# Later, source-ordered splits of two summed operands of the output projection, and one small step of the tail moved

## The chip, the core and the metric

The kernel runs on one core of a Trainium2 chip. The metric is the device time of one launch in microseconds; of several runs the median is given. TensorE is called PE, VectorE DVE, ScalarE ACT, GpSimd POOL and SyncE SP, as in the profile.

## The reference

A trunk of two layers over 1024 tokens of width 1024. The first is a gMLP layer with chunks of 128 tokens; the second is attention in a sliding window of 128 tokens, with 16 query heads of size 64 on 4 shared key/value heads, sinks and ALiBi. The change touches only the second layer's end. Cut to that:

```python
q, z = jnp.split(h @ w_in, 2, axis=-1)
# per block of 128 tokens: logits = q k^T + alibi, masked to the window
p = jnp.exp(logits - m[..., None])
denom = jnp.sum(p, axis=-1) + jnp.exp(sink - m)
o = einsum(p, v) / denom
y = (o * jax.nn.silu(z)) @ w_out
h = h + rms_norm(y, b_post_g)
```

Everything is float32.

## The kernel before, in words

*Products.* A float32 operand is split into a high part (an ACT copy to fp32r, L105) and a low part (a DVE subtraction, L106). `mm3` (L215 to L218) then makes three fp32r matmuls: high by high, high by low, low by high. The large products use Strassen's scheme with seven block products instead of eight, so sums and differences of operand blocks have to be formed and split too.

*Stages.* First the gMLP layer (v, then u and z, then its output projection), then q, the first half of z, the keys and values. After that, `attn` runs 16 units of attention (8 blocks of tokens in two groups p of heads) and weaves into them, in small steps, a list of other PE work called `fill`: the rest of z and q, and at the end `Out.early`, the first five block products of the output projection. `Out.late`, the last two block products and the finals, runs after the units.

*A unit.* `scores` makes the logits of 8 heads in four PSUM banks with the tag "s" (matmuls L1155), then on DVE masks each bank (L1162, COPY_PREDICATED) and takes bias and row maximum twice per bank (L1169, tile mx). `exps` runs on ACT (L1175), `normalise` on DVE in two halves (L1181, L1182, tile pr), `transposes` on PE (L1189, tile pt), with ACT copies (L1191) and POOL selections (L1194, L1195). `values` multiplies by v (L1218, tile o, again two "s" banks, so it needs banks that the masks and maxima have set free), and `gate` multiplies by z on DVE (L1230, L1231). There are four "s" banks in all.

*The output projection.* In `early` the products go in the order oc (twice), od, oe with the summed operand o1, oe with o7. Each product has 8 steps (two weight blocks u, four token blocks t), so there are 40 steps, numbered from 0: od is steps 16 to 23, the o1 product 24 to 31, the o7 product 32 to 39. Each step is six matmuls.

*The two summed operands.* o1 and o7 each hold four token blocks. For each block, the plan SUMS names (m, t, step of the load, step of the sum, step of the split): the gated output of a unit of the first four blocks is loaded again from memory (`y_again`, a raw tile), POOL adds that of a unit of the last four blocks (L253), and the sum is split into o1 or o7. Source order of the steps is the order of this table, but the scheduler may move instructions on an engine; `held` ties the instructions of the units on DVE and ACT to their source order, and leaves those of `fill` free. o1 and o7 lie in the space of q's first half (tags P0a and P0b), which the oc products read.

*Raw buffers.* The raw tiles (tag "raw") have three buffers. They are shared by the loads for o1 and o7, by the two weight blocks of product 3 that are split on the chip (w46 and w47, from wo_b; the other output weights were split earlier and kept in memory), and by three of the residual loads for the finals. The sums for o1 go to another tile, so their raw tile is free after the sum; those for o7 stay in the raw tile until the split.

*The tail.* `late` makes product of (L216 to L218, tile of) in two parts, and for each token block adds, scales by the gain on DVE or POOL, and finishes with the residual (L1309). ef holds the mean squares: four columns are prepared at once (L1447, 128x4), then one per token block (L1461).

Of the kernel before, what the change touches and what calls it, by code (L numbers as in the profile page):

```python
# [7 lines left out]
F32 = mybir.dt.float32  # L8
# [3 lines left out]
AF = mybir.ActivationFunctionType  # L12
ALU = mybir.AluOpType

P = 128
D = 1024
# [8 lines left out]
EPS = 1e-6  # L25
# [25 lines left out]
def tile_yoco(  # L51
# [19 lines left out]
    nc = tc.nc  # L71
# [9 lines left out]
    def bank(tag, name):  # L81
        return psum.tile([P, 512], F32, tag=tag, name=name)
# [21 lines left out]
    def split(hi, lo, src):  # L104
        nc.scalar.activation(hi, src, AF.Copy)  # L105
        nc.vector.tensor_tensor(lo, src, hi.bitcast(F32), ALU.subtract)  # L106
# [19 lines left out]
    class Weights:  # L126
# [30 lines left out]
        def load(self, i):  # L157
            for n in range(min(len(self.raw), 20), min(i, 19) + 1):
                src, kind = self.order[n]
                if n < 20:  # L160
                    self.raw[n] = wload(src, f"w{n}")
# [48 lines left out]
    def wnext():  # L210
        w = weights.get()
        weights.ahead()
        return w
# [38 lines left out]
    def add(out, a, b, op, eng=None):  # L252
        (eng or nc.vector).tensor_tensor(out, a, b, op)  # L253
# [820 lines left out]
    def by_head(t):  # L1074

        return t.rearrange("p k t -> p (k t)").rearrange("p (m b g t) -> p m b g t", m=4, g=2, t=P)
# [204 lines left out]
    ORDER = "01FavFbgmtpFFn"  # L1281
    lags = {}
    BY = [6, 12, 19, 25, 32, 38, 45, 51, 57, 64, 71, 78, 85, 92, 99, 106, 112, 120]
    SUMS = [(1, 0, 0, 2, 17), (1, 1, 3, 5, 18), (1, 2, 6, 8, 19), (7, 0, 8, 11, 18), (1, 3, 10, 12, 20), (7, 1, 14, 16, 21), (7, 2, 19, 21, 24), (7, 3, 23, 25, 28)]
    behind = {}

    def held(what, *args):
# [31 lines left out]
    def y_again(p, t):  # L1319
        r = raw_tile(f"y{p}_{t}_{len(again)}")  # L1320
        again[len(again)] = r
        load(r[:, 0:512], yd[p][t])
        return r[:, 0:512]

    class Out:
# [26 lines left out]
        def sums(self, plan):  # L1352
            todo = {}
            for m, t, *at in plan:
                for what in range(3):
                    todo.setdefault(at[what], []).append((what, m, t))
            raw = {}
            for at in range(max(todo) + 1):
                for what, m, t in todo.get(at, ()):
                    if what == 0:  # L1360
                        raw[m, t] = y_again(m == 1, t)
                    elif what == 1:
                        d = self.s1[t] if m == 1 else raw[m, t]
                        mix = [a.rearrange("p (a t) -> p a t", t=P) for a in (d, raw[m, t])]
                        add(mix[0], mix[1], self.z[0][:, :, t * P:(t + 1) * P], ALU.add, nc.gpsimd)
                        raw[m, t] = d
                    else:
                        if m not in self.o:
                            self.o[m] = big.tile([P, 2, 4, 4, P], F32R, tag={1: "P0a", 7: "P0b"}[m], name=f"o{m}")
                        split(*(self.o[m][:, e, t].rearrange("p m t -> p (m t)") for e in range(2)), raw[m, t])  # L1370
                yield

        def early(self):
# [31 lines left out]
            def products():  # L1405
                ps = [bank("mm", f"oc{t}") for t in range(4)]
                yield from self.product(ps, self.of(self.q0, 0), True, True, lambda t, p: copy(m4[t], p))
                yield from self.product(ps, self.of(self.q0, 1), False, True, after2)
                ps = [bank("mm", f"od{t}") for t in range(4)]
                yield from self.product(ps, self.of(self.q1, 0), True, True, after5)  # L1410
                ps = [bank("mm", f"oe{t}") for t in range(4)]
                yield from self.product(ps, sum_operand(1), True, True,
                                        lambda t, p: add(n2[t], n2[t], p, ALU.add))
                yield from self.product(ps, sum_operand(7), False, True, after7)

            sums = self.sums(SUMS)
            for _ in products():
                step(sums)
                yield

        def late(self):
            gp, n2, m5, q1 = self.gp, self.n2, self.m5, self.q1
            ps = [bank("s", f"of{t}") for t in range(4)]

            def after3(t, p):
                c = m5[t]
                add(c, c, p, ALU.add)
                self.square(1, 0, t, c)
                add(c, c, gp[0], ALU.mult, nc.gpsimd)

            for k, _ in enumerate(self.product(ps, self.of(q1, 1), True, False, after3)):
                if k < 4:
                    d = self.z[1][:, :, k * P:(k + 1) * P]
                    hi, lo = (by_head(w)[:, 0:2, k] for w in q1)
                    split(hi, lo, d.rearrange("p (m g) t -> p m g t", m=2))
                elif k == 4:
                    w = [wnext() for _ in range(2)]
                    for dst, src in self.stores:
                        tc.keep_in_program_order(nc.sync.dma_start(out=dst, in_=src))
                elif k == 5:  # L1440
                    final(*self.rest.pop(0))
                elif k == 6:
                    hf = big.tile([P, 4, D], F32, tag="P0a", name="hf1")
                    xt = [load(hf[:, t], h1d[1][t]) for t in range(4)]
            final(*self.rest.pop(0))
            ef = const.tile([P, 8], F32, tag="rpa", name="ef1")
            nc.vector.tensor_scalar(ef[:, 0:4], self.ss[1][:, 0], 1.0 / D, EPS, ALU.mult, ALU.add)  # L1447
            y = self.of(q1, 0)
            for t in range(4):
                for m in range(4):  # L1450
                    hi, lo = w[m // 2]
                    cs = slice(m % 2 * 512, m % 2 * 512 + 512)
                    a = y(t, m)
                    mm3(ps[t], a[0], a[1], hi[:, cs], lo[:, cs], False, m == 3)
                c, o, r = n2[t], self.m4[t], ef[:, 4 + t:5 + t]
                add(c, c, ps[t], ALU.add)
                self.square(1, 1, t, c)
                add(o, c, gp[1], ALU.mult)
                if t:
                    final(*self.rest.pop(0))  # L1460
                nc.vector.tensor_scalar(r, self.ss[1][:, 1, t:t + 1], 1.0 / D, ef[:, t:t + 1], ALU.mult, ALU.add)  # L1461
                nc.gpsimd.tensor_tensor(r, r, nhalf[:, 0:1], ALU.pow)
                self.rest.append((1, t, [m5[t], o], r, xt[t]))
            final(*self.rest.pop(0))
# [85 lines left out]
```

## Time and profile before

| | |
|---|---|
| median of 3 runs | 1044.87 us (1043.71 to 1045.28) |
| the profiled execution | 1044.52 us |
| its span, first to last instruction | 1042.8 us |
| mean granted PE clock | 0.993 |
| PE busy | 1025.3 us (98%) |
| DVE busy | 792.4 us (76%) |
| ACT busy | 541.1 us (52%) |
| POOL busy | 276.2 us (26%) |

The span lies inside the execution's own time. A row of a timeline gives the start and the length in us, the engine, the line, the operation, the tiles written and read, and in brackets the idle time of the engine before it with what ended it. Where instructions follow each other without a wait, the next starts somewhat ahead of the end of the one before, since they overlap in the engine. A row with x2 merges two.

### The profile page before, as it was taken

The page shows a single profiled execution, that of the slowest core. Times are in us where ns is not written, and L with a number is a line of the kernel's source. Part 1 is how long each engine was busy: PE and PEld are TensorE (multiplying, and loading weights), DVE is VectorE, ACT ScalarE, POOL GpSimd, SP SyncE. Part 2 cuts the span into 40 slices and gives each one's busy share as a digit, 9 for nine tenths or more (in the row PEclk, how much of TensorE's full clock was granted, in tenths as well). Part 3 has the DMA queues.
Part 4 walks back from the last instruction along what each step waited for, and adds up shares of the span by engine and source line. Part 5 has one row for each costly group of instructions (what it writes and reads, how often), then busy time and mean ns, then how long its engine had stood idle before and what let it go on. Part 6 is the DMA issues. An engine that isn't in the chain of part 4 may idle for free.

```text
span 1042.8 us, 14527 instructions
## 1 busy us (share of the span) xinstructions
PE 1025.3 (98%) x5186; PEld 839.6 (81%) x5186; DVE 792.4 (76%) x1342; ACT 541.1 (52%) x1018; POOL 276.2 (26%) x257
## 2 busy tenths in 40 slices
PE   9999999999999999999999999999999999999896
PEld 7888788888888888888878888888987777777575
DVE  6987467899898998988697777655166658787778
ACT  6684444565665565755445465444145445556332
POOL 0000004384664755743200000000001113244244
PEclk9999999999999999999999999999999999999898
DMA  8877353445555455457998651996135544334465
GB/s 313 273 277 287 101 175 116 151 152 176 173 162 172 134 184 157 157 176 254 316 388 311 203 203 53 349 352 241 51 143 190 176 149 142 112 106 146 173 222 202
DMA packets 117672, 203.83 MB, mean 195 GB/s; under 512 B 7776, under 2 KB 59872, under 8 KB 117600
## 3 DMA queue, kind: packets, MB, share of 16 engines
q1 hardware_dynamic: 113088, 194.22, 54.4%
q10 hardware_dynamic: 4512, 8.68, 2.4%
q8 instruction: 41, 0.67, 0.3%
q14 instruction: 31, 0.25, 0.1%
HBM read 142.05 MB, written 60.82 MB: 195 GB/s over the span
## 4 chain that ended last, share of the span: by engine, by line
PE 74%; DVE 7%; DMA 7%; issue 5%; ACT 3%; POOL 2%; SPq 1%; POOLq 0%; DVEq 0%; ACTq 0%
PE qz L216 5%; PE ub L216 5%; PE ub L218 5%; PE ub L217 5%; PE qz L218 5%; PE qz L217 5%; PE sp L659 2%; PE uc L217 2%; PE uc L216 2%; PE uc L218 2%; PE o L1218 2%; PE s L1155 2%; PE ob L218 2%; PE ob L216 2%; PE ob L217 2%
## 5 line engine op out<-in xcount | busy, mean ns | idle before, releaser
L1175 ACT ACTIVATE pr<-pr,mx 128x129 f32<-128x129 f32 x128 | 50.2, 394 | 56.3 <-DVE mx L1169 56.2
L216 PE MATMUL qz<-n_hi,whi_w 128*128 128x512 f32 x192 | 77.3, 403 | 0.0
L218 PE MATMUL qz<-n_hi,wlo_w 128*128 128x512 f32 x192 | 75.1, 391 | 0.1
L217 PE MATMUL qz<-n_lo,whi_w 128*128 128x512 f32 x192 | 74.9, 390 | 0.0
L803 POOL TENSOR_TENSOR presum<-presum_raw 128x128 f32<-128x128 f32 x80 | 49.1, 645 | 91.9 <-DMA od<-presum 84.8
L110 DVE SCALAR_TENSOR_TENSOR wlo_w<-raw_w,gn,whi_w 128x512 fp32r<-128x512 f32 x40 | 28.7, 748 | 48.6 <-ACT whi_w L109 48.5
L109 ACT ACTIVATE whi_w<-raw_w,gn 128x512 fp32r<-128x512 f32 x40 | 27.1, 715 | 63.2 <-PE pv L218 30.4
L253 POOL TENSOR_TENSOR f<-raw_uz 128x512 f32<-128x512 f32 x15 | 20.3, 1356 | 124.4 <-DMA raw_uz<-in_wuz_in_dram 105.6
L1195 POOL TENSOR_SCALAR_AFFINE_SELECT pc<-pc 128x1024 f32<-128x1024 f32 x16 | 20.1, 1259 | 121.6 <-DVE wlo_w L110 108.8
L216 PE MATMUL ub<-T,uzhilo_g 128*128 128x512 f32 x128 | 50.7, 396 | 0.9 <-ACT uz_slots L256 0.9
L106 DVE TENSOR_TENSOR uzhilo_g<-f,uzhilo_g 128x1024 fp32r<-128x1024 f32 x31 | 47.3, 1526 | 5.4 <-ACT uzhilo_g L105 5.4
L216 PE MATMUL ub<-T,whi_g 128*128 128x512 f32 x128 | 50.8, 397 | 0.0
L812 DVE TENSOR_TENSOR presum<-presum 128x128 fp32r<-128x128 f32 x80 | 50.6, 681 | 0.1
L218 PE MATMUL ub<-T,wlo_g 128*128 128x512 f32 x128 | 50.0, 391 | 0.0
L218 PE MATMUL ub<-T,uzhilo_g 128*128 128x512 f32 x128 | 49.9, 390 | 0.0
L217 PE MATMUL ub<-T,uzhilo_g 128*128 128x512 f32 x128 | 49.9, 390 | 0.0
L217 PE MATMUL ub<-T,whi_g 128*128 128x512 f32 x128 | 49.9, 390 | 0.0
L105 ACT ACTIVATE uzhilo_g<-f 128x1024 fp32r<-128x1024 f32 x31 | 32.8, 1057 | 32.2 <-PE uc L218 25.9
L216 PE MATMUL uc<-T,uzhilo_g 128*128 128x512 f32 x124 | 49.0, 395 | 0.0
L256 ACT ACTIVATE uz_slots<-ub 128x512 f32<-128x512 f32 x48 | 28.2, 587 | 39.7 <-PE ub L218 37.4
L217 PE MATMUL uc<-T,uzhilo_g 128*128 128x512 f32 x124 | 48.3, 390 | 0.0
L218 PE MATMUL uc<-T,uzhilo_g 128*128 128x512 f32 x124 | 48.3, 390 | 0.0
(399 smaller groups left out, 3301.0 us busy)
## 6 DMA issues: line engine op xcount, KB each, us to landing
raw_uz<-in_wuz_in_dram SPq DMA_DIRECT2D x32, 512.0 KB, 3.7
td<-uz_slots SPq DMA_DIRECT2D x56, 256.0 KB, 2.2
orawP2a<-td SPq DMA_DIRECT2D x28, 512.0 KB, 4.3
od<-presum SPq DMA_DIRECT2D x16, 640.0 KB, 4.0
raw<-in_wv_in_dram SPq DMA_DIRECT2D x17, 512.0 KB, 5.5
vg<-vd SPq DMA_DIRECT2D x8, 1024.0 KB, 5.6
orawP2b<-in_wo_a_dram SPq DMA_DIRECT2D x16, 512.0 KB, 8.0
raw_w<-in_wqz_dram SPq DMA_DIRECT2D x16, 512.0 KB, 5.1
```

The source lines that it names most:

```text
L105: nc.scalar.activation(hi, src, AF.Copy)
L106: nc.vector.tensor_tensor(lo, src, hi.bitcast(F32), ALU.subtract)
L109: nc.scalar.activation(hi, src, AF.Copy, scale=g)
L110: nc.vector.scalar_tensor_tensor(lo, src, g, hi.bitcast(F32), ALU.mult, ALU.subtract)
L216: nc.tensor.matmul(out, lhsT=a_hi, rhs=b_hi, start=start, stop=False, skip_group_check=True)
L217: nc.tensor.matmul(out, lhsT=a_hi, rhs=b_lo, start=False, stop=False, skip_group_check=True)
L218: nc.tensor.matmul(out, lhsT=a_lo, rhs=b_hi, start=False, stop=stop, skip_group_check=True)
L256: nc.scalar.activation(out, a, AF.Copy)
L659: nc.tensor.matmul(psv[:, n], lhsT=d["vg"][:, 4 * j + n, i * P:(i + 1) * P], rhs=d["wc"], start=True, stop=True)
L803: tc.keep_in_program_order(nc.gpsimd.tensor_tensor(o, a, b, op))
L812: tc.keep_in_program_order(nc.vector.tensor_tensor(t[:, k], lo[k], hi.bitcast(F32), ALU.subtract))
L1175: nc.scalar.activation(pr[:, i], pr[:, i], AF.Exp, bias=mx[:, i:i + 1], scale=-1.0, accum_out=dn[:, i:i + 1])
```

## The change

Four edits. The table SUMS moves the splits later: those of o1 from steps 17, 18, 19, 20 to 18, 20, 22, 23, those of o7 from 18, 21, 24, 28 to 25, 27, 29, 31. The last o7 block is also loaded at step 26, not 23, and summed at 27, not 25. The two instructions of each of these splits are now held at their place in the source. In the tail the step that prepares ef for four blocks moves behind the first block's add and gain.

```diff
-    SUMS = [(1, 0, 0, 2, 17), (1, 1, 3, 5, 18), (1, 2, 6, 8, 19), (7, 0, 8, 11, 18), (1, 3, 10, 12, 20), (7, 1, 14, 16, 21), (7, 2, 19, 21, 24), (7, 3, 23, 25, 28)]
+    SUMS = [(1, 0, 0, 2, 18), (1, 1, 3, 5, 20), (1, 2, 6, 8, 22), (7, 0, 8, 11, 25), (1, 3, 10, 12, 23), (7, 1, 14, 16, 27), (7, 2, 19, 21, 29), (7, 3, 26, 27, 31)]
...
-                        split(*(self.o[m][:, e, t].rearrange("p m t -> p (m t)") for e in range(2)), raw[m, t])
+                        hi, lo = (self.o[m][:, e, t].rearrange("p m t -> p (m t)") for e in range(2))
+                        tc.keep_in_program_order(nc.scalar.activation(hi, raw[m, t], AF.Copy))
+                        tc.keep_in_program_order(
+                            nc.vector.tensor_tensor(lo, raw[m, t], hi.bitcast(F32), ALU.subtract))
...
             ef = const.tile([P, 8], F32, tag="rpa", name="ef1")
-            nc.vector.tensor_scalar(ef[:, 0:4], self.ss[1][:, 0], 1.0 / D, EPS, ALU.mult, ALU.add)
...
                 add(o, c, gp[1], ALU.mult)
-                if t:
+                if t == 0:
+                    nc.vector.tensor_scalar(ef[:, 0:4], self.ss[1][:, 0], 1.0 / D, EPS, ALU.mult, ALU.add)
+                else:
                     final(*self.rest.pop(0))
```

The first place is DVE, before, from the last sum of product oc to the first mask of the last unit's scores (s_1_00, of block 8 and the second group of heads); o_8285 is o1, o_8296 is o7, pr_1_8131 belongs to the unit before:

```order
L106 TENSOR_TENSOR o_8285<-sum_P2b,o_8285 128x512 x2
L106 TENSOR_TENSOR o_8296<-raw_yFalse_3_8106,o_8296 128x512
L1181 RECIPROCAL dn_1_8133<-dn_1_8133 128x4
L106 TENSOR_TENSOR o_8285<-sum_P2b,o_8285 128x512
L1182 TENSOR_TENSOR pr_1_8131<-pr_1_8131,dn_1_8133 128x4x128
L1134 COPY pr_1_8301<-snk 128x8
L106 TENSOR_TENSOR o_8285<-sum_P2b,o_8285 128x512
L106 TENSOR_TENSOR o_8296<-raw_yFalse_5_8225,o_8296 128x512
L106 TENSOR_TENSOR o_8296<-raw_yFalse_6_8353,o_8296 128x512
L1162 COPY_PREDICATED s_1_00_8305<-mrg,s_1_00_8305 128x2x64
```

The same place now, where o_8291 is o1:

```order
L1373 TENSOR_TENSOR o_8291<-sum_P2b,o_8291 128x512
L1181 RECIPROCAL dn_1_8133<-dn_1_8133 128x4
L1182 TENSOR_TENSOR pr_1_8131<-pr_1_8131,dn_1_8133 128x4x128
L1134 COPY pr_1_8296<-snk 128x8
L1162 COPY_PREDICATED s_1_00_8300<-mrg,s_1_00_8300 128x2x64
```

Seven splits stood ahead of the mask, and the eighth after the second mask; now one stands there, and none among the masks and maxima.

The second place is DVE from the next q_lo split on, up to the sums of od, before (pr_1_8301 is the last unit's):

```order
L106 TENSOR_TENSOR q_lo<-z_0_5648,q_hi 128x2x256
L1181 RECIPROCAL dn_1_8303<-dn_1_8303 128x4
L1182 TENSOR_TENSOR pr_1_8301<-pr_1_8301,dn_1_8303 128x4x128
L253 TENSOR_TENSOR sum_P_3_7908<-sum_P_3_7908,od_8267 128x512
L253 TENSOR_TENSOR sum_P_3_7908<-sum_P_3_7908,od_8268 128x512
```

And now (pr_1_8296 is the last unit's, o_8454 is o7):

```order
L106 TENSOR_TENSOR q_lo<-z_0_5648,q_hi 128x2x256
L253 TENSOR_TENSOR sum_P_3_7908<-sum_P_3_7908,od_8267 128x512
L1373 TENSOR_TENSOR o_8291<-sum_P2b,o_8291 128x512
L1181 RECIPROCAL dn_1_8298<-dn_1_8298 128x4
L253 TENSOR_TENSOR sum_P_3_7908<-sum_P_3_7908,od_8268 128x512
L1373 TENSOR_TENSOR o_8291<-sum_P2b,o_8291 128x512
L1373 TENSOR_TENSOR o_8454<-raw_yFalse_3_8106,o_8454 128x512
L1182 TENSOR_TENSOR pr_1_8296<-pr_1_8296,dn_1_8298 128x4x128
```

Both sums and three splits came to stand ahead of pr's second half; on PE the transposes that read it moved three matmuls later in product oe.

The third place is SP's queue, before, from the load of the last o7 block on:

```order
L270 DMA raw_yFalse_7_8439<-yd_3_5286 128x512
L101 DMA raw_w_8514<-in_wo_b_dram 128x1024
L101 DMA raw_w_8567<-in_wo_b_dram 128x1024
L270 DMA raw_hf_0_8611<-h1d_0_72 128x1024
L150 DMA wlo_w_8371<-od_88 128x1024
```

And now, with the loads of kept weights (L150) that lay behind:

```order
L150 DMA wlo_w_8364<-od_88 128x1024
L150 DMA whi_w_8363<-od_88 128x1024
L150 DMA wlo_w_8439<-od_87 128x1024
L150 DMA whi_w_8438<-od_87 128x1024
L270 DMA raw_yFalse_7_8498<-yd_3_5286 128x512
L150 DMA wm_w_8509<-od_88 128x1024 x2
L101 DMA raw_w_8512<-in_wo_b_dram 128x1024
L101 DMA raw_w_8567<-in_wo_b_dram 128x1024
L270 DMA hf_8746<-h1d_0_76 128x1024
```

The two weight loads (L101) moved behind six loads of kept weights, and the last o7 load behind four of them.

## The prediction

> **What bounds the kernel now.** First the page. Its slices say that the array is busy from end to end, and that its clock is lowered in one slice before the last:
>
> ```profile
> PEclk9999999999999999999999999999999999999898
> ```
>
> Then the windows of 5 us around that slice (columns: stretch, its length, PE, PEld, DVE, ACT and POOL busy with instructions, granted clock, DMA share, GB/s):
>
> ```profile
> 965.00:970.00 5.00, 4.21 (x35) 3.03 (x34) 5.00 (x12) 1.25 (x3) 0.00 (x0) 1.00 0.38 129
> 970.00:975.00 5.00, 1.67 (x10) 0.53 (x12) 4.19 (x18) 1.99 (x8) 1.47 (x1) 0.95 0.70 231
> 975.00:980.00 5.00, 5.00 (x19) 2.88 (x12) 2.36 (x9) 2.04 (x9) 0.59 (x1) 0.50 0.81 311
> 980.00:985.00 5.00, 5.00 (x25) 4.16 (x24) 3.31 (x5) 3.66 (x8) 3.15 (x4) 0.87 0.00 0
> ```
>
> PE stops near 969, has 1.67 us of work in the next 5 us, and then runs at half clock while DVE was full (5.00 of 5). The waits of PE over the whole kernel name the cause:
>
> ```profile
> PE o L1218 <- DVE mx L1169: 4.1, 2, 3.0
> PE vb L216 <- ACT vhi L105: 0.8, 1, 0.8
> ```
>
> So PE's only large wait is for the score maxima on DVE, before the value products "o" of one unit. PE's timeline shows a clean round of this work (first two rows), the disturbed one, and the start of the next product:
>
> ```profile
> 954.96 0.40 PE L218 MATMUL oc<-wm_w,q_lo 128*128 128x512 f32 x1
> 959.60 1.03 PE L1189 MATMUL pt<-ident,pr 128*128 128x128 f32 x8
> ...
> 968.81 0.40 PE L218 MATMUL od<-whi_w,q_lo 128*128 128x512 f32 x1
> 972.23 1.08 PE L1218 MATMUL o<-pc,vt 64*64 64x512 f32 x4 [3.02 <-DVE mx L1169]
> 974.41 1.93 PE L1218 MATMUL o<-pp,vt 64*64 64x512 f32 x8 [1.11 <-DVE mx L1169]
> 977.12 0.79 PE L216 MATMUL od<-whi_w,q_hi 128*128 128x512 f32 x1
> 981.92 1.04 PE L1189 MATMUL pt<-ident,pr 128*128 128x128 f32 x8
> 985.54 0.39 PE L216 MATMUL oe<-wm_w,o 128*128 128x512 f32 x1
> ...
> 988.26 1.03 PE L1189 MATMUL pt<-ident,pr 128*128 128x128 f32 x8
> ```
>
> From the last matmul ahead of "o" to the transposes "pt" the clean round takes 959.60 - 954.96 = 4.64 us, the disturbed one 981.92 - 968.81 = 13.11. The loss is **8.47 us**: 3.02 + 1.11 waited, 4.34 from the lowered clock. DVE's timeline shows what stood ahead of the maxima:
>
> ```profile
> 961.99 1.58 DVE L1182 TENSOR_TENSOR pr<-pr,dn 128x512 f32<-128x512 f32 x1
> 966.18 1.28 DVE L106 TENSOR_TENSOR o<-sum_P2b,o 128x512 fp32r<-128x512 f32 x2
> 969.93 1.28 DVE L106 TENSOR_TENSOR o<-raw_yFalse,o 128x512 fp32r<-128x512 f32 x2
> 971.13 0.28 DVE L1162 COPY_PREDICATED s<-mrg,s 128x128 f32<-128x128 uint32 x1
> 972.00 0.29 DVE L1162 COPY_PREDICATED s<-mrg,s 128x128 f32<-128x128 uint32 x1
> 973.03 0.69 DVE L106 TENSOR_TENSOR o<-raw_yFalse,o 128x512 fp32r<-128x512 f32 x1 [0.74 <-ACT o L105]
> 973.64 0.35 DVE L1169 CUSTOM_DVE_ANT_0 pr<-s,bias,snk 128x128 f32<-128x128 f32 x1
> ```
>
> Seven splits of o1 and o7 run at 966.18 to 971.13, and the eighth cuts the chain of maxima in two (its operand comes late: 0.74 waited). These are the splits that the change moves.
>
> **The change part by part.**
>
> *Splits.* No arithmetic is added or removed: eight ACT copies and eight DVE subtractions stay. The first place of the order shown with the change says what moves. Between the last sum of product "oc" and the first mask (L1162) of the last unit's scores one split is left of seven, and none inside the maxima. From 966.18 I count split 0.6 (half of a pair's row of 1.28), reciprocal 0.2, pr 0.6, copy 0.1: the first mask starts at 967.7, not 971.13. In the row of before PE started 972.23 - 971.13 = 1.10 after the mask; 968.8 now, when PE comes only at 968.81 + 0.3 (its switch to "o"), 969.1. The second bank takes 0.87 (971.13 to 972.00) + 0.33 + 0.77 (973.64 to 974.41) = 1.97: 969.7, against 969.1. I keep **0.5 us** of wait (bounds 0 and 0.9). So 8.47 goes and 0.5 stays.
>
> What is late next: pr of the last unit (its second half), which the next "pt" reads. By the second place of the order, two sums and three splits now stand ahead of it on DVE. Prices and POOL's part:
>
> ```profile
> 977.92 0.69 DVE L1230 TENSOR_TENSOR pc<-o,pc 128x512 f32<-128x512 f32 x1 [1.90 <-ACT pc L1223]
> 980.72 0.69 DVE L253 TENSOR_TENSOR sum_P<-sum_P,od 128x512 f32<-128x512 f32 x1 [1.38 <-ACT sum_P2b L256]
> 981.53 1.08 DVE L1182 TENSOR_TENSOR pr<-pr,dn 128x512 f32<-128x512 f32 x1
> 963.09 1.43 POOL L1195 TENSOR_SCALAR_AFFINE_SELECT pc<-pc 128x1024 f32<-128x1024 f32 x1
> 970.86 1.47 POOL L253 TENSOR_TENSOR raw_yFalse<-raw_yFalse,z 128x512 f32<-128x512 f32 x1 [6.34 <-DMA raw_yFalse<-yd]
> ```
>
> The four banks of maxima (0.87 each) end at 971.2. The gate waits for "o" and its ACT copy, 971.8, and takes 1.5: 973.3. Then a sum 0.6, the second o1 split beside POOL's two z steps 1.3 (between 0.6 and the 1.58 row), reciprocal and sum 0.8, pr's first half 1.1, q_lo 1.3: 978.4. Sum, split, reciprocal, sum 2.0: 980.4. Two splits and pr 1.9: 982.3; PE follows at 982.4. PE reaches this "pt" after "oe" (985.54 - 8.47 + 0.5 = 977.6) and now 15 matmuls, 0.227 each (12 in 988.26 - 985.54): 981.0. A new wait of **1.4 us** (bounds 0.3 with all DVE work at clean prices, 2.4 with two more steps at 1.58).
>
> [...]
>
> *Loads.* The o7 splits hold their raw buffers longer, and the two late weight loads share these three buffers. By the third place of the order, the weight loads went behind six loads of kept weights on SP, and wait for the second and third o7 split. Their time from issue to landing, in the view of DMA issues:
>
> ```profile
> raw_w<-in_wo_b_dram SPq DMA_DIRECT2D x2, 512.0 KB, 3.9
> ```
>
> And the rows of the timelines that this touches:
>
> ```profile
> 970.63 0.98 SPq L101 DMA_DIRECT2D raw_w<-in_wo_b_dram  x2
> 997.06 0.89 DVE L106 TENSOR_TENSOR q_lo<-z,q_hi 128x512 fp32r<-128x512 f32 x1 [1.24 <-ACT q_hi L105]
> 1000.30 1.23 DVE L106 TENSOR_TENSOR wlo_w<-raw_w,whi_w 128x1024 fp32r<-128x1024 f32 x1 [0.40 <-ACT whi_w L105]
> 1008.56 1.28 DVE L253 TENSOR_TENSOR sum_P<-sum_P,oe 128x512 f32<-128x512 f32 x2
> 1011.56 0.39 PE L216 MATMUL of<-whi_w,q_hi 128*128 128x512 f32 x1
> 1011.91 1.77 DVE L1309 SCALAR_TENSOR_TENSOR sum_P<-sum_P,ef,raw_hf 128x512 f32<-128x512 f32 x1 [0.76 <-POOL ef L1303]
> 1015.84 0.75 DVE L1309 SCALAR_TENSOR_TENSOR sum_P<-sum_P,ef,raw_hf 128x512 f32<-128x512 f32 x1 [0.46 <-POOL ef L1303]
> 1018.88 0.15 DVE L1301 TENSOR_SCALAR ef<-ssb 128x1 f32<-128x1 f32 x1 [0.85 <-ACT junk_b L1350]
> 1026.45 1.25 DVE L1447 TENSOR_SCALAR ef<-ssb 128x4 f32<-128x4 f32 x1
> 1024.47 3.21 POOL L253 TENSOR_TENSOR sum_P2b<-sum_P2b,gpb 128x512 f32<-128x512 f32 x2 [0.34 <-ACT junk_b L1350]
> 1027.62 0.67 DVE L253 TENSOR_TENSOR sum_P2a<-sum_P2a,of 128x512 f32<-128x512 f32 x1
> ```
>
> All behind "pt" shifts by -8.47 + 0.5 + 1.4 = -6.6. The q_lo split is over at 997.95 - 6.6 = 991.3; the second o7 split beside POOL 1.2: 992.5; landing 3.9 later, 996.4; ACT's copy about 1.1; so the DVE weight split starts at 997.5, not 1000.30 - 6.6 = 993.7. PE needs it at 1011.56 - 6.6 = 1005.0, so PE is covered by over 6 us. DVE is not: the last gate and everything down to the tail's sums stand behind that split, 3.8 us later against PE. Idle that absorbs it: 0.76 + 0.46 + 0.85 = 2.1 us. Left: **+1.7** (bounds 0 and 3.8).
>
> *The small step.* ef 128x4 took 1.25 us beside POOL's multiplications, which end at 1027.68; the sum behind it started at 1027.62, although its matmuls were done by about 1025.2 (60 from 1011.56 on, 0.227 each). Put behind that sum and the product by gpb (0.6 each), it meets POOL's end and costs 0.2: **-1.0** (bounds -1.2 and 0, since PE may then be what DVE waits for). Nothing is moved on a queue by it.
>
> **Sum.** -8.47 + 0.5 + 1.4 + 1.7 - 1.0 = -5.9 us. The profiled execution took 1044.52 us, 1.7 around its span of 1042.8; it becomes 1038.6. The median of the runs shown is 1044.87, 0.35 higher: **1039.0**. A measurement of this kernel can tell about 0.2%, 2.1 us, from no change.
>
> **The rivals.**
> - *The lags vanish* (chance 0.18): DVE's clean prices hold, "pt" waits 0.3 and the tail is bound by PE: -8.47 + 0.3 + 0.3 + 0 - 1.0 = -8.9, 1036.0. For it: DVE idles 1.90 and 1.38 us in the rows above. Against: its row of pr beside POOL.
> - *The clock falls again* at the new wait (0.10). The second window's 0.95 puts the fall at 974.5; in the 3.4 us before it PE worked 1.08 + 0.1 us; a wait of 0.8 us left the clock alone. 1.4 us lies between. Half clock for 6.8 us as before (0.5 + 5 + 1.3 by the three windows) would cost 3.4: 1042.4. [...]
> - *The stall only moves* (0.04, the slower side): at "pt" all three splits, the sums and pr run at 1.58, not 0.6, beside POOL. That adds 6 x 0.98 = 5.9 to the 1.4; from about 3 us on the clock halves too (4.34). -8.47 + 0.5 + 7.3 + 4.34 + 1.7 - 1.0 = +4.4: 1049.3. Against: POOL's selections take 1.43 and are over about when the first of these steps starts.
> - *No effect* (0.04): the maxima are late for another reason than the splits: 1044.9. Against: up to 970 DVE was busy 5.00 us of 5, mostly with splits.
>
> **How the numbers follow.** The forecast itself has 0.64. Its own bounds reach from the first rival, 1036.0, to 1039.0 + 2.1 (the whole tail lag unabsorbed) + 0.6 (half of "pt"'s upper bound) = 1041.7; between them lie 0.64 + 0.18 and some of the second rival. Faster by over 0.2% (below 1042.8): 0.64 + 0.18 + 0.10 = 0.92; same 0.04; slower 0.04.
>
> **What would show it.** Right: no row of "o" waiting for mx over 1 us, clock 1.00 from 965 to 985, a wait of PE at "pt" for pr L1182 of about 1.4 us, raw_w loads issued near 992 and not 15 us ahead, the ef row at 0.2. Wrong: half clock in any window there, PE waiting for wlo_w at "of", or a second large wait for mx.

## The result, and the profile after

The changed kernel takes 1040.71 us (median of 15 runs, 1038.98 to 1045.48), beside 1045.99 for the kernel before, measured with it (15 runs, 1043.71 to 1049.71). The ratio is 0.9957, with a 95% interval of 0.9942 to 0.9971: faster by 4.5 us (3.0 to 6.1). The ratio goes by the means; between the medians it is 5.3 us. The profiled execution takes 1040.13 us against 1044.52, so 4.39 less; its span is 1038.4 us, its mean granted clock 0.998.

The windows of 5 us around the old stall (columns as before) in the changed kernel:

```profile
965.00:970.00 5.00, 5.00 (x43) 3.56 (x44) 4.90 (x18) 0.93 (x5) 0.00 (x0) 1.00 0.26 103
970.00:975.00 5.00, 5.00 (x35) 3.60 (x32) 4.03 (x14) 4.26 (x17) 1.29 (x1) 1.00 0.60 213
975.00:980.00 5.00, 5.00 (x25) 4.17 (x24) 5.00 (x7) 4.44 (x9) 4.55 (x3) 1.00 0.22 70
980.00:985.00 5.00, 3.56 (x31) 2.21 (x29) 2.70 (x6) 0.00 (x0) 0.28 (x1) 1.00 0.55 194
```

PE is busy through the place where it had 1.67 us of work in five, and the clock stays at 1.00. A hole of 1.44 us is left in the last of the four. The waits of PE:

```profile
PE of L216 <- DMA whi_w<-od: 1.5, 1, 1.5
PE pt L1189 <- DVE pr L1182: 1.4, 1, 1.4
```

The row of "o" waiting for the maxima is gone, and the wait for pr is there as forecast. The wait for a weight block (whi_w) at the product "of" is one that I did not forecast. The same in PE's timeline:

```profile
969.12 0.40 PE L218 MATMUL od<-whi_w,q_lo 128*128 128x512 f32 x1
969.44 1.08 PE L1218 MATMUL o<-pc,vt 64*64 64x512 f32 x4
...
974.24 1.03 PE L1189 MATMUL pt<-ident,pr 128*128 128x128 f32 x8
...
982.85 1.06 PE L1189 MATMUL pt<-ident,pr 128*128 128x128 f32 x8 [1.44 <-DVE pr L1182]
...
1005.48 0.39 PE L216 MATMUL of<-whi_w,q_hi 128*128 128x512 f32 x1
...
1019.79 0.50 PE L216 MATMUL of<-whi_w,q_hi 128*128 128x512 f32 x1 [1.50 <-DMA whi_w<-od]
```

From the last matmul ahead of "o" (969.12) to the transposes (974.24) it is 5.12 us, against 13.11 before and 4.64 in a clean round. DVE's timeline, from the first mask of the last unit to the end:

```profile
967.97 0.29 DVE L1162 COPY_PREDICATED s<-mrg,s 128x128 f32<-128x128 uint32 x1
...
982.02 0.68 DVE L1182 TENSOR_TENSOR pr<-pr,dn 128x512 f32<-128x512 f32 x1
987.06 0.69 DVE L1230 TENSOR_TENSOR pc<-o,pc 128x512 f32<-128x512 f32 x1 [4.36 <-ACT pc L1223]
...
998.97 1.23 DVE L106 TENSOR_TENSOR wlo_w<-raw_w,whi_w 128x1024 fp32r<-128x1024 f32 x1 [1.70 <-ACT whi_w L105]
...
1021.09 1.78 DVE L1309 SCALAR_TENSOR_TENSOR sum_P2a<-sum_P2a,ef,hf 128x512 f32<-128x512 f32 x1
...
1024.49 0.15 DVE L1462 TENSOR_SCALAR ef<-ssb 128x4 f32<-128x4 f32 x1
...
1034.61 0.75 DVE L1309 SCALAR_TENSOR_TENSOR sum_P<-sum_P,ef,hf 128x512 f32<-128x512 f32 x1
```

And the two rows of before that answer to the third last and the last of these:

```profile
1024.76 1.78 DVE L1309 SCALAR_TENSOR_TENSOR sum_P2a<-sum_P2a,ef,hf 128x512 f32<-128x512 f32 x1
...
1039.00 0.75 DVE L1309 SCALAR_TENSOR_TENSOR sum_P<-sum_P,ef,hf 128x512 f32<-128x512 f32 x1
```

SP's rows in the changed kernel show the raw weight loads behind the splits, at 994.30 and no longer at 970.63:

```profile
994.30 1.57 SPq L101 DMA_DIRECT2D raw_w<-in_wo_b_dram  x2
```

So the account of the profiled pair is this. PE's product "of" starts at 1005.48, not 1011.56: 6.08 earlier, although this execution had come 0.31 later to the place (969.12 against 968.81). At the row of 1021.09 DVE is only 3.67 ahead of before (1024.76): 2.41 of PE's 6.08 are lost again on DVE. From that row to the last one it is 13.52 us, before 14.24: 0.72 come from the small ef step. 6.08 - 2.41 + 0.72 = 4.39, the measured difference.

### The profile page after: what moved, and what is told of

The parts are those of the page before. It is cut to its first block, busy times and chain, and to the rows that moved or that the text cites. A ratio compares the mean times of both kernels' runs of the same rounds, so it can differ in the third digit from the quotient of the medians.

```text
span 1038.4 us, 14533 instructions
## 1 busy us (share of the span) xinstructions
PE 1023.2 (99%) x5186; PEld 838.3 (81%) x5186; DVE 791.2 (76%) x1342; ACT 541.8 (52%) x1018; POOL 272.6 (26%) x257
## 4 chain that ended last, share of the span: by engine, by line
PE 74%; DVE 10%; issue 5%; DMA 5%; ACT 3%; POOL 2%; SPq 1%; DVEq 0%; POOLq 0%; ACTq 0%
PE ub L216 5%; PE qz L216 5%; PE ub L218 5%; PE ub L217 5%; PE qz L218 5%; PE qz L217 5%; PE uc L216 3%; PE uc L217 2%; PE uc L218 2%; PE oc L216 2%; PE oc L218 2%; PE sp L659 2%; PE oc L217 2%; PE o L1218 2%; PE s L1155 2%
## 5 line engine op out<-in xcount | busy, mean ns | idle before, releaser
L803 POOL TENSOR_TENSOR presum<-presum_raw 128x128 f32<-128x128 f32 x80 | 43.2, 574 | 91.1 <-DMA od<-presum 84.1
```

The lines of the kernel that those rows point to most:

```text
L803: tc.keep_in_program_order(nc.gpsimd.tensor_tensor(o, a, b, op))
```

## The experiments

The theory: the gain is the stall at "o" (about 8 us), and what eats part of it is DVE's lag in the tail, which comes from the late raw weight loads, and the new wait at pt. The rivals: the whole gain is in the order of the table, or in holding the splits, or in ef; the waits that are left cost nothing; or the clock costs more than the waits. Each time below stands beside runs of the kernel before on the same chip, which had medians of 1045.65 to 1046.69; so kernels are compared by their ratios.

**The parts of the change alone.** Only the new table, with the splits free:

```diff
-    SUMS = [(1, 0, 0, 2, 17), ... (7, 3, 23, 25, 28)]
+    SUMS = [(1, 0, 0, 2, 18), ... (7, 3, 26, 27, 31)]
```

> Only the new step numbers, nothing held at its place in the source. Theory (the pins move the splits, the numbers say where to): the scheduler still puts all seven early splits ahead of the last unit's masks, so PE waits about 3 us at the value products, the clock halves for about 6.8 us, and the time is that of before within 1 us. Rival (the numbers do the work): the wait goes and the time falls by 4 to 6 us.

1044.65 us, ratio 0.9975 (0.9961 to 0.9988). Its DVE timeline has the same seven splits ahead of the first mask as before, since the scheduler put them back, and PE waits for the maxima:

```profile
967.88 1.28 DVE L106 TENSOR_TENSOR o<-sum_P2b,o 128x512 fp32r<-128x512 f32 x2
969.09 1.88 DVE L106 TENSOR_TENSOR o<-raw_yFalse,o 128x512 fp32r<-128x512 f32 x3
970.90 0.28 DVE L1162 COPY_PREDICATED s<-mrg,s 128x128 f32<-128x128 uint32 x1
...
974.54 0.69 DVE L106 TENSOR_TENSOR o<-raw_yFalse,o 128x512 fp32r<-128x512 f32 x1 [1.83 <-ACT o L105]
```

```profile
PE o L1218 <- DVE mx L1169: 3.0, 1, 3.0
```

There is one wait instead of two. The eighth split still stands among the masks and waits longer for its operand (974.54, 1.83 us idle), but now behind the maxima of the second bank; "o" needs two banks, so it no longer waits for this split. The table alone does not do what its numbers say.

The time missed the expectation of before within 1 us, and the half clock that it expected is absent from the profiled execution: there the clock stays at 1.00 behind the wait of 3.02 us, and the execution takes 1039.86 us, 4.8 less than the median of the twelve runs. The three runs with a mean clock of 0.996 or 0.997 take 1039.86, 1042.92 and 1041.37 us, the nine with 0.993 to 0.995 between 1043.14 and 1047.75. So where its clock is not lowered, this kernel, with its stall but with its weight loads early (970.39), comes near the changed one, and where it is, near the one before; the last section has the rows on the clock.

Only the holding, with the old table:

```diff
-                        split(*(self.o[m][:, e, t] ...), raw[m, t])
+                        tc.keep_in_program_order(nc.scalar.activation(hi, raw[m, t], AF.Copy))
+                        tc.keep_in_program_order(nc.vector.tensor_tensor(lo, raw[m, t], ...))
```

> The old step numbers with every split held in source order; the small tail step unmoved. Three splits stand ahead of the last unit's masks, one between the sums and pr. Theory (each split ahead of the masks costs PE 0.6 us, each ahead of pr 0.6 us): a wait at the value products of 1 to 2 us without half clock, a wait at the transposes below 0.5 us, the weight loads earlier than in the changed kernel, 5 to 7 us faster than before. Rival (the longer leads are needed): the wait at the value products stays near 3 us, the clock halves, and the gain is under 2 us.

1043.93 us, ratio 0.9977 (0.9964 to 0.9989). The waits of PE in its profile:

```profile
PE pt L1189 <- DVE pr L1182: 2.1, 1, 2.1
PE o L1218 <- DVE mx L1169: 0.8, 1, 0.8
```

The expectation of a wait below 0.5 us at pt failed. Two more splits stand ahead of the masks than in the changed kernel, so the maxima come 1.2 us later (the mask follows the first half of the unit before's pr by 6.88 us, not 5.68), and pr comes later with them. And the granted clock fell behind the wait of 2.1 us (0.50 from 985.00 to 988.41). So holding takes the long stall away, and the table decides how large the waits are that remain. That both are needed is shown by these rows and not by the times: holding alone has 0.9977, and the changed kernel with ef at its old place (below), which has holding and table, 0.9968 (0.9955 to 0.9982). Holding alone issues its weight loads 9.3 and 14.2 us behind the first mask, the changed kernel from 26.3 on, and the next runs show what that costs.

Only the small step (the diff of before, ef moved):

> Before with the small tail step moved alone. Theory (DVE sets the end, and the step of 1.25 us shrinks to 0.2): 1.0 us faster than before. Rival (PE sets the end, DVE waits for it): no difference, within 0.3 us.

1045.69 us, ratio 0.9991 (0.9977 to 1.0005): 0.9 us, not told from nothing by itself. In its profile the step takes 0.16 us, and the two rows that lay 14.24 us apart before lie 13.52 apart (1031.64 and 1045.16). The other way round, the changed kernel with ef at its old place:

> The changed kernel with the small tail step at its old place. Theory: the step takes about 1.2 us again beside POOL's multiplications, DVE is late from its stage on, and the kernel is 1.0 us slower than the changed one, so about 4 us faster than before. Rival: the same time as the changed one within 0.3 us, since its tail already waits for PE and its weights.

1042.53 us, ratio 0.9968 (0.9955 to 0.9982), against 0.9957 with it. Its profile shows the step at its old price:

```profile
1026.38 1.78 DVE L1309 SCALAR_TENSOR_TENSOR sum_P2a<-sum_P2a,ef,hf 128x512 f32<-128x512 f32 x1
1028.09 1.25 DVE L1450 TENSOR_SCALAR ef<-ssb 128x4 f32<-128x4 f32 x1
...
1040.63 0.74 DVE L1309 SCALAR_TENSOR_TENSOR sum_P<-sum_P,ef,hf 128x512 f32<-128x512 f32 x1
```

From the first of these rows to the last it is 14.25 us, in the changed kernel 13.52: 0.73, the same as against before. The intervals of the two ratios overlap, so it is the rows that carry this.

**Is the wait at pt on the path, and are the loads?** For these I compare, in each profile, the stretch from the first mask of the last unit on DVE to the end of DVE's last row; up to the mask DVE's order is the same. In the changed kernel it is 67.39 us (967.97 to 1035.36).

The value products of the unit before the last put ahead of the transposes, so that PE has work while pr is made:

```diff
-            for what in ORDER if i < len(units) else "tvgpFFFF":
+            for what in ORDER if i < len(units) else "vtgpFFFF":
```

> The changed kernel, with the value products of unit u14 put ahead of the transposes of u15 in the tail of attention (order vtgp instead of tvgp). DVE's work up to pr is the same; PE has the 1.45 us of value products to do while it would wait. Theory (the 1.44 us wait at pt is a real loss that stands on the path): the wait at pt falls to 0.4 us or less, the gate of u14 starts about 3 us earlier on DVE, the raw weight loads follow it by about 2 us, and the time falls by 1.1 us at least, 2.5 at most: 1038.2 to 1039.6. Rival (the tail on DVE, late for its own reason, sets the end and the wait at pt is hidden behind it): the wait at pt goes and the time stays at 1040.7 within 0.5 us.

1040.30 us, ratio 0.9945 (0.9932 to 0.9958). PE's row at pt:

```profile
988.02 1.06 PE L1189 MATMUL pt<-ident,pr 128*128 128x128 f32 x8 [0.67 <-DVE pr L1182]
```

0.77 of the wait went, and PE's "of" starts 0.97 us earlier behind the mask (36.54 us, in the changed kernel 37.51), but the stretch fell by 0.46 only (973.14 to 1040.07, 66.93 us). The rival is nearer by the median, but this kernel does not test it cleanly. Its DVE tail, from the first weight split on, has the order of the kernel before. The changed kernel and its variants with ef at the old place and with hf late (below) have another order there, in which the second weight split stands behind a sum; no edit asks for either. So a comparison with the changed kernel mixes the edit with that order.

Then the loads alone: the second and third o7 split put behind pr, where DVE was idle for 4.36 us. (This kernel was run last, so its expectation draws on runs that follow here.)

```diff
-    SUMS = [..., (7, 1, 14, 16, 27), (7, 2, 19, 21, 29), (7, 3, 26, 27, 31)]
+    SUMS = [..., (7, 1, 14, 16, 26), (7, 2, 19, 21, 26), (7, 3, 26, 27, 31)]
...
-            for what in ORDER if i < len(units) else "tvgpFFFF":
+            for what in ORDER if i < len(units) else "FtvgpFFF" if i == len(units) else "tvgpFFFF":
...
-            if e in PINS or what.__name__ != "more" and e in UP:
+            if e in PINS or (what.__name__ != "more" or args == (16, 0)) and e in UP:
```

> The changed kernel, with only the second and third split of o7 put into DVE's idle time behind pr; the transposes stay ahead of the value products, but the scheduler puts three more matmuls of oe ahead of them, so that about 0.8 of the 1.44 us of wait at pt is left. Theory (the late raw loads alone make the tail late): raw loads issued near 984, DVE ends about 6.3 us behind the last matmul, no wait of PE at of, 0.8 us more from the first mask of the last unit to the end than in the kernel with both edits in order (63.7), 64.5 against 67.4 in the changed kernel: 1037.5 to 1038.5. Rival (both edits are needed, one alone is hidden by the other loss, as the value products alone gave only 0.5): 1039.7 to 1040.7.

1038.81 us, ratio 0.9943 (0.9926 to 0.9960). SP and DVE:

```profile
984.27 0.97 SPq L101 DMA_DIRECT2D raw_w<-in_wo_b_dram  x2
```

```profile
968.90 0.29 DVE L1162 COPY_PREDICATED s<-mrg,s 128x128 f32<-128x128 uint32 x1
...
1032.96 0.75 DVE L1309 SCALAR_TENSOR_TENSOR sum_P<-sum_P,ef,hf 128x512 f32<-128x512 f32 x1
```

The loads go out 15.4 us behind the mask, not 26.3; the stretch is 64.81 us, 2.58 less, and PE waits nowhere at "of". The wait at pt is 0.72, since three more matmuls stand ahead of it; by them PE's "of" starts 0.69 earlier behind the mask (36.82). The other 1.89 is DVE's lag: from the start of "of" (1005.72) to DVE's end it takes 27.99 us, in the changed kernel 29.88. So the raw loads are the larger loss, as the theory had it (the time lies 0.3 above its range), although this DVE tail has the order of before. Their price in one and the same order is read from the last two kernels below.

Both edits (to the diff just shown comes the order of value products and transposes; "the run before" in the expectation is the one with the value products first), first with the value products of the last unit where the scheduler put them (twelve matmuls later), then at their old place:

```diff
-            for what in ORDER if i < len(units) else "tvgpFFFF":
+            for what in ORDER if i < len(units) else "FvtgpFFF":
```

> As the run before, and the second and third split of o7 put between pr and the gate of u14 on DVE, where it was idle for 4.36 us, and held there; the fourth block is loaded one step earlier in source order. So the weights' raw buffers come free at about 984 us and not at 992 to 994. Theory (the tail lag of 2.4 us behind PE comes from the late raw loads): loads issued near 984, DVE's weight split no longer after 997, no wait of PE at of, the tail's sums follow PE: 1.4 for pt and 2.4 for the lag go, about 1037.0. Rival (the tail is bound by the amount of DVE work or by the crowded DMA queues, whatever the loads do): no better than the run before by more than 0.5 us, 1038.5 to 1039.5.

1038.62 us, ratio 0.9933 (0.9921 to 0.9946); the stretch is 65.17 us. By the time that is the rival's range. The loads go out at 983.59 and PE waits nowhere behind the mask, as the theory had it, but DVE ends 7.78 us behind the start of the last matmul (in the changed kernel 6.15): the later value products delay the last gate, and with it DVE's splits of q_lo.

```diff
-            for what in ORDER if i < len(units) else "FvtgpFFF":
+            for what in ORDER if i < len(units) else "FvtgpFFF" if i == len(units) else "vgpFFFF":
```

> As the kernel with both edits (value products ahead of the transposes, second and third split of o7 in DVE's idle time), with the value products of the last unit at their old place ahead of the product oe with o7, and not twelve matmuls later, where the scheduler had put them; with that DVE's splits of q_lo come early again as well. In the kernel with both edits PE waited nowhere behind 965 us, and DVE ended 7.8 us behind the last matmul, against 5.9 with the wait of 3.3 us at pt. Theory (that difference of 1.9 us is DVE work in a worse order, and PE bounds the tail otherwise): DVE ends 5.9 to 6.5 us behind the last matmul, 1.2 to 1.9 us less than the kernel with both edits, 1036.7 to 1037.4. Rival (the DVE work of the tail takes as long in either order): the same as the kernel with both edits, 1038.2 to 1039.0.

1038.48 us, ratio 0.9931 (0.9914 to 0.9948). DVE:

```profile
967.26 0.29 DVE L1162 COPY_PREDICATED s<-mrg,s 128x128 f32<-128x128 uint32 x1
...
1030.22 0.74 DVE L1309 SCALAR_TENSOR_TENSOR sum_P<-sum_P,ef,hf 128x512 f32<-128x512 f32 x1
```

The stretch is 63.70 us, 1.47 less than the run before and 3.69 less than the changed kernel; DVE ends 6.3 us behind the last matmul, as the theory had it. The time missed the theory's 1036.7 to 1037.4, and the medians do not tell the last two kernels apart. The profiled execution is the shortest of all, 1035.73 us. Its interval and that of the changed kernel (0.9942 to 0.9971) overlap from 0.9942 to 0.9948, so that it is faster than the changed kernel is likely and not certain. Against the kernel with the loads alone, whose order is the same on DVE from the first weight split on and on PE behind the last value products, "of" starts 0.97 earlier and the stretch is 1.11 shorter: with the loads early, the last 0.72 us of wait at pt stood on the path.

**The wait for whi_w at "of".** The four loads of hf for the second half go behind the last weight loads on SP:

```diff
+                    hf = big.tile([P, 4, D], F32, tag="P0a", name="hf1")
+                    xt = [hf[:, t] for t in range(4)]
+                    for t in range(4):
+                        tc.keep_in_program_order(nc.sync.dma_start(out=xt[t], in_=h1d[1][t]))
                     for dst, src in self.stores:
...
-                elif k == 6:
-                    hf = big.tile([P, 4, D], F32, tag="P0a", name="hf1")
-                    xt = [load(hf[:, t], h1d[1][t]) for t in range(4)]
```

> The changed kernel, with the four loads of hf for the second half (2 MB) put behind the loads of the last two weight blocks on SP, and held there; no other engine's order changes. In the changed kernel's profile they go out from 996 to 1002 us, the transfers are full from 1000 to 1020, and PE waits 1.5 us for whi_w at of. Theory (DVE is busy without a break from 1013 to 1031, so the end hangs on DVE and PE's wait costs nothing): the wait at of goes, the time stays, 1040.4 to 1041.0. Rival (PE's wait delays the sums on DVE and stands on the path): the wait goes and the time falls by 1 to 1.5 us, 1039.2 to 1039.7.

1042.22 us, ratio 0.9964 (0.9951 to 0.9977), so slower than either side expected. The wait is gone, DVE's order is that of the changed kernel, and nothing is gained; the stretch is 67.86 us (969.32 to 1037.18). PE's last matmul is earlier, and DVE ends 8.6 us behind it. In the changed kernel PE's wait of 1.5 us stood on no path: DVE set the end.

**At what wait does the clock fall?** PE's order held, so that PE waits longer at pt with the same work on DVE:

```diff
-            if e in PINS or what.__name__ != "more" and e in UP:
+            if e in PINS or e == "PE" and (what.__name__ == "transposes" or what.__name__ == "more" and args[0] > 14) or what.__name__ != "more" and e in UP:
```

> The changed kernel, with PE's instructions of the last two rounds of attention held in source order, so that three matmuls of oe (0.68 us) come behind the transposes pt and not ahead of them. DVE's order up to pr is the same, so PE waits about 2.1 us at pt and not 1.44. It asks at which wait the clock falls. Theory (a wait of 2.1 us leaves the clock alone): clock 1.00 from 980 to 990, DVE is no later than it was, time as the changed kernel, 1040.5 to 1041.2. Rival (the clock falls at a wait of 2 us, as it did once with only the splits held and the old plan): half clock for 3.4 us, 1.7 us lost on PE, 1041.5 to 1042.5.

1044.53 us, ratio 0.9983 (0.9975 to 0.9992). PE waited 2.12 us, the clock stayed at 1.00 in the profiled execution (981.22 to 988.05), and yet the stretch grew by 2.1 us: in the tail the scheduler had put DVE's steps back into the order of before, and PE waited 1.31 us for a sum there. So the price of this kernel says nothing of the clock. With the second and third o7 split ahead of pr as well:

```diff
-    SUMS = [..., (7, 1, 14, 16, 27), (7, 2, 19, 21, 29), (7, 3, 26, 27, 31)]
+    SUMS = [..., (7, 1, 14, 16, 25), (7, 2, 19, 21, 25), (7, 3, 26, 27, 31)]
```

> As the run before, and the second and third split of o7 ahead of pr as well: pr is 1.2 us later, and PE waits about 3.3 us at pt; the raw weight loads come about 10 us earlier. Theory (above about 3 us the clock halves, and the tail lag of 2.4 us comes from the late loads): half clock for 3.4 to 6.8 us behind pt (1.7 to 3.4 us lost), gate 1.2 us later, lag of the tail gone: 1040.7 + 1.2 + 2.5 - 2.4 = 1042.0. Rival without the fall of the clock: 1039.5. Rival in which the lag does not come from the loads: 1044.4.

1041.20 us, ratio 0.9953 (0.9941 to 0.9964). The wait at pt is 3.32 us, the longest of all, and the clock did not fall (1.00 from 980.20 to 990.44). This kernel gives pr 1.2 us later than the one before it and ends 2.7 us earlier (its stretch is 66.82 us, against 69.48): its raw loads go out 14.8 us behind the mask, not 26.3. The time is nearest to the theory's 1042.0, but the fall of the clock in that figure did not happen. From the first weight split on, the order on DVE is the same in these two kernels, and so is PE's behind the last value products. So this pair shows best what the loads cost. Here are PE's first "of" and DVE's last row, first of the kernel whose loads are late, then of the one whose loads are early:

```profile
1008.24 0.39 PE L216 MATMUL of<-whi_w,q_hi 128*128 128x512 f32 x1
...
1038.79 0.74 DVE L1309 SCALAR_TENSOR_TENSOR sum_P<-sum_P,ef,hf 128x512 f32<-128x512 f32 x1
```

```profile
1008.60 0.39 PE L216 MATMUL of<-whi_w,q_hi 128*128 128x512 f32 x1
...
1035.30 0.74 DVE L1309 SCALAR_TENSOR_TENSOR sum_P<-sum_P,ef,hf 128x512 f32<-128x512 f32 x1
```

From "of" to DVE's end it is 31.29 us with the loads late and 27.44 with them early, so late loads cost 3.85 us in this order of DVE's steps. With them late, DVE stands idle for 1.68 us ahead of the first weight split, for ACT's copy of the loaded block; with them early it does not wait there. The kernel before, whose loads are early too, has 28.19, or 27.47 without its 0.72 for the ef step. The changed kernel has 29.88: with its own order of DVE's tail only 2.4 us are lost.

## Why the prediction was right

*The stall at "o"* (-8.47, and +0.5 left). Measured 13.11 to 5.12 us, against 4.64 clean: 0.48 is left. It appears in no row of waits, since the "o" block only runs longer (969.44 to the next product at 971.39), but the size and the cause are the ones forecast: the second half of the block starts at 969.95, behind the second bank's maxima, which end at 969.80 (forecast 969.7). Two readings on the way were wrong and leave the sum alone. The prediction put 4.34 us of the loss down to the lowered clock; by its own three windows, 6.8 us at half clock, that is 3.4, and the rest lies in the "o" block, which ran in pieces. And DVE was full in the window ahead of the half clock, not during it (2.36 of 5).

*The wait at pt* (+1.4). Measured 1.44 by the mechanism given: sums and splits ahead of pr, some beside POOL. My prices for the steps beside POOL (1.3 for the split, 1.1 for pr's half) came near the 1.10 and 1.12 us measured, but they were taken as fixed prices, and in the rows of the last section the length goes with the end of POOL's step; that part is luck. PE's "of" should start 6.57 earlier; it started 6.08 earlier, and 0.31 of that difference was there ahead of the place.

*The tail lag* (+1.7, bounds 0 and 3.8). The cause held: loads issued at 994.30 ("near 992"), the weight split on DVE at 998.97 (forecast 997.5), DVE late against PE. The size is 2.41 by the rows of 1024.76 and 1021.09, so this term was mis-sized by 0.7, and its second half by a wrong mechanism.

The weight split came 4.75 us late against PE, not 3.8: 1.33 ahead of before (1000.30), while "of" came 6.08 ahead. The prediction let all work behind pt shift with PE. But the last gate but one and the q_lo split follow pt, which itself had moved behind three more matmuls (0.68 us, counted in its 15): the gate came 5.38 earlier (987.06, before 992.44). That is 0.7 of the difference. The o7 split of 992.49 took 1.77 us and not 1.2, beside a POOL step that had begun at 992.00 (last section), which is 0.5; from its end to the weight split it was 4.7 and not 5.0.

Then 2.34 were absorbed, near the 2.1 counted, but not for the reason given. The prediction counted 0.76, 0.46 and 0.85 us of idle time in before's order of DVE's tail. In the kernel with PE held and late loads, which has that order but for the ef step, the same three idle times are still there (0.82, 0.46 and 0.85), and the lag is 3.8 to 3.9. They follow steps of POOL and ACT that are late with DVE, and absorb next to nothing. In the changed kernel the scheduler had put DVE's tail in another order, in which of these idle times only 0.32 is left. So the size came near by luck.

*The small step* (-1.0). Measured -0.72 and, by the kernel without it, -0.73. The step itself fell from 1.25 to 0.15 us as forecast, but the product by gpb, now ahead of it, stood beside POOL's in its place (1.08 us at 1023.49; the next, at 1025.60, took 0.69).

*The sum.* -8.47 + 0.48 + 1.44 + 2.41 - 0.72 = -4.86, and 0.31 from before the place, against the forecast of -5.9 and the measured -4.39 of the profiled pair (0.16 are spread over PE's rows). The forecast of 1039.0 is 1.7 below the median, within the range of 1036.0 to 1041.7; as a gain, 5.9 were forecast, and 5.3 between the medians or 4.5 by the ratio were measured, since the runs of before made with it were 1.1 above those shown. The errors of size lie in the lag (0.7) and in the small step (0.3), both to the slow side; the one mechanism that was wrong is the idle time that was to absorb the lag.

*What else the runs say of it.* It treated the wait at pt and the tail lag as terms that add. With the loads early, taking the last 0.72 us of wait at pt away shortened the stretch by 1.1, so the wait counts in full there. With the loads late, taking 0.77 away gave 0.46, but in another order of DVE's tail; how much of the wait the lag hides is not shown. It named a wait at "of" for wlo_w as a sign that it is wrong; a wait for the other half of another block, whi_w, did appear, from crowded transfers (DMA share 1.00 from 1015 to 1020; it went when the loads of hf were put behind), and cost nothing. Of the rivals, *the lags vanish* gave 1036.0; the last kernel with both edits comes near it in its profiled execution, 1035.73, but not in its median, 1038.48. *The clock falls again* did not happen at 1.44 us (1.00 in all four windows). *The stall only moves* has the clock halve from about 3 us on; the runs show no such length, since it stayed at 1.00 at 3.02 us (table alone) and 3.32 us and fell at 2.09.

## What to carry to other kernels

When a step is moved off an engine's critical chain, follow its buffers as well: here the splits that were moved held raw buffers, and the weight loads behind them took back 2.4 of 8 us in a stage some 20 us later. A table of due times did not move these splits while the scheduler was free to put them back, and holding them at the old due times left a wait of 2.1 us; the order has to be read after both, also far behind the place that was edited, since the scheduler may change it there too. Idle time in a row absorbs a delay only if what the engine waits for is not delayed with it. And a wait on one engine is worth removing only if no other engine is already late behind it, as the 1.5 us at "of" show: one run that removes it by itself tells.

## What the runs showed of the hardware

*DVE beside POOL.* The changed kernel's rows show what these steps took. DVE:

```profile
973.84 0.69 DVE L253 TENSOR_TENSOR sum_P<-sum_P,od 128x512 f32<-128x512 f32 x1 [0.22 <-ACT sum_P2b L256]
974.44 1.10 DVE L1373 TENSOR_TENSOR o<-sum_P2b,o 128x512 fp32r<-128x512 f32 x1
...
976.13 1.12 DVE L1182 TENSOR_TENSOR pr<-pr,dn 128x512 f32<-128x512 f32 x1
977.17 1.57 DVE L106 TENSOR_TENSOR q_lo<-z,q_hi 128x512 fp32r<-128x512 f32 x1
...
992.49 1.77 DVE L1373 TENSOR_TENSOR o<-raw_yFalse,o 128x512 fp32r<-128x512 f32 x1
```

and POOL:

```profile
973.71 1.29 POOL L253 TENSOR_TENSOR z<-z,z 128x512 f32<-128x512 f32 x1 [8.88 <-DVE z L1231]
975.07 1.62 POOL L253 TENSOR_TENSOR z<-sum_P2b,z 128x512 f32<-128x512 f32 x1
976.66 1.54 POOL L1194 TENSOR_SCALAR_AFFINE_SELECT pp<-pc 128x1024 f32<-128x1024 f32 x1
...
992.00 1.72 POOL L253 TENSOR_TENSOR z<-sum_P2b,z 128x512 f32<-128x512 f32 x1
```

All but the sum read two SBUF tiles. These four end at 975.54, 977.25, 978.74 and 994.26: each 0.54 to 0.56 us behind the end of the POOL step that they met (975.00, 976.69, 978.20, 993.72), however late they came. Each row is as long as what was left of POOL's step when it began, and 0.54 to 0.56 us more. The sum with od, which reads a PSUM bank, took 0.69 us beside the POOL step of 973.71. The row of 1.08 of before (981.53 to 982.61), which the prediction took as a price, began 0.53 us ahead of the end of POOL's step, at 982.06:

```profile
980.77 1.29 POOL L253 TENSOR_TENSOR z<-sum_P2b,z 128x512 f32<-128x512 f32 x1
```

In these five rows, 1.08 to 1.77 us long, the length is no fixed factor; it goes with the time at which POOL's step ended.

*The clock.* In these runs the length of a wait does not tell whether the granted clock falls. In the execution of before it is at 0.50 for 6.83 us from 974.49 on, behind waits of 3.02 and 1.11 us, and again from 1035.93 on, when PE has stopped (its last matmul begins at 1033.10); in that of the kernel with ef moved alone it falls at 537.67 and 977.99. The windows here are 3.41 us long, the shortest stretch at half clock in these rows (985.00 to 988.41 below), and are counted back from the last fall of each execution. For the kernel before (columns as in the windows above; PE busy is the third number, the granted clock the one with two decimals behind POOL):

```profile
967.66:971.08 3.42, 1.55 (x6) 0.94 (x6) 3.42 (x8) 0.00 (x0) 0.22 (x1) 1.00 0.29 77
971.08:974.49 3.41, 1.16 (x8) 0.33 (x12) 2.62 (x13) 1.48 (x6) 1.25 (x1) 1.00 0.81 286
974.49:977.90 3.41, 3.41 (x14) 1.46 (x15) 1.47 (x9) 1.41 (x7) 0.00 (x0) 0.50 0.98 342
```

of the kernel with the splits held and the old table, whose wait was 2.09 us:

```profile
981.59:985.00 3.41, 1.32 (x9) 0.89 (x8) 2.77 (x6) 0.00 (x0) 0.00 (x0) 1.00 0.79 263
985.00:988.41 3.41, 3.41 (x22) 1.40 (x20) 0.00 (x0) 0.00 (x0) 0.00 (x0) 0.50 0.52 205
```

and of the one that waited 3.32 us at pt:

```profile
980.20:983.61 3.41, 1.78 (x8) 1.13 (x6) 3.41 (x7) 1.77 (x4) 0.74 (x1) 1.00 0.80 303
983.61:987.02 3.41, 1.72 (x16) 1.22 (x20) 1.54 (x3) 0.00 (x0) 0.83 (x1) 1.00 0.72 229
987.02:990.44 3.42, 3.42 (x24) 2.38 (x17) 0.90 (x2) 1.57 (x3) 0.43 (x1) 1.00 0.42 155
```

The wait of 3.32 us lies half in the first and half in the second of these windows (PE idle for 1.63 and 1.69 us), and the clock stayed at 1.00; the wait of 2.09 lies in one window, and the clock was at 0.50 for the 3.41 us behind it. Cut in the same way, the wait of 3.02 us in the kernel with the table alone gives idle of 1.90 and 1.12 us, and that of 2.12 (PE held) 1.82 and 0.30, and the clock stayed at 1.00 behind both. In the windows just ahead of the falls, up to PE's end, PE was idle for 2.25 us (before), 2.09 (splits held, old table), 2.61 and 2.04 (ef moved alone), and 1.76 (ef at its old place, 533.19 to 536.60, at another stage of the kernel). So a wait of 2.09 us was followed by half clock, and waits of 2.12, 3.02 and 3.32 us in other executions were not; what sets the clock is not shown. Nor is it shown how long it stays low: 3.41 us (splits held, old table), 6.83 (before) and 10.24 (ef moved alone, from 977.99) were seen, and the work in them does not tell why.
